# Token stages of a two-layer hybrid block: from a scheduler's order to an order written out, with split work spread over the products

## The chip, the cores and the metric

The kernel runs on one core of one Trainium2 chip. The metric is device time in microseconds of one execution. The program is built through a tile framework: the kernel text emits instructions, the framework's scheduler puts the instructions of each engine into one fixed order, and on the chip each engine issues its own instructions in that order and waits on semaphores for the others. TensorE (PE), VectorE (DVE), ScalarE (ACT) and GpSimd (POOL) compute; the queue of SyncE (SP) issues every transfer.

## The reference, cut to what matters

Two layers of a hybrid block over 1280 tokens (256 of context, 1024 latent) of width 1024. In each layer a normalised and modulated input goes through one input projection, whose columns feed three branches: a bidirectional state-space scan (SSD), grouped-query attention (GQA), and differential attention. The outputs go through one output projection, are normalised and added to the stream.

```python
def ssd_branch(...):
    xs, bs, cs, dt_f, dt_b = prep(p)            # depthwise conv, SiLU, softplus
    y_lf, _ = ssd_scan(xl, dlf, a_f, bl, cl, s_f)                 # chunks of 128 tokens
    y_lb, _ = ssd_scan(flip(xl), flip(dlb), a_b, flip(bl), flip(cl), s_b)
    y = yf + flip(yb_rev) + xs * d_skip[:, None]
    return rmsnorm(y * silu(z), norm_g)
def gqa_branch(...):      # per-head RMSNorm of q and k, axial rotary, softmax attention, SiLU gate
def diff_branch(...):     # rotary on q and k, two softmax maps, o1 - lam * o2, RMSNorm, SiLU gate
```

## The kernel before, in words

The 1280 tokens are ten tiles of 128. Products in float32 accuracy are made of three matmuls: each operand is split into a high part (rounded to fp32r) and a low part (the rest, `lo_part`, L126 to L128), and hi*hi, hi*lo and lo*hi are summed in PSUM.

A layer has these stages, in the order in which they are emitted:

1. Products with channels on partitions for conv inputs (`t_block`, L572), the depthwise conv (`conv_tile`, L599), step sizes (`dt_part`, L492), and splitting of the output weights.
2. The token stages (L909 to L1113), which the change is about. `tok_chunk` (L939) takes one block of columns of the projection, called a chunk of weights here: 0 is z, 1 is dq and dk, 3 is dv (256 columns), 2 is gq, gk and gv, 4 is the gates. For each chunk it loads the eight k-tiles of the weights (L943, three landing buffers `wf`), splits them into `wh` (ACT, L947) and `wl` (DVE for even k, POOL for odd k, L948; nine buffers each), and then, for each token tile, makes 24 matmuls into one of two PSUM banks `prj` (L954 to L960) and works off the bank at once: tanh and a multiply for the SiLU (L963, L964), or a copy (L977), rotary (`rope`, L875), norms (`gqa_norm`, L890), splits (`qk_split`, L825), PE transposes into another bank (`qk_transpose`, L838), an ACT copy out of it (L843) and stores through SP.
3. While chunks 0, 1 and 3 run, the generator `scan` (L753) is advanced by 1.3 steps per full product (`SCR`). For each of ten token tiles it does a forward step and a backward step of the SSD. The forward step loads `ab`, a broadcast of decays (L762, 1 MB, one buffer), makes masked C*B products (L767 to L770), 16 DVE instructions on `ab` (L773, L774), an exponential (L776), eight ACT and eight DVE instructions (L779, L780), one POOL product (L782), eight products (L790), and adds parts; state updates are in `state_step` (L705). The first of the two directions to reach a tile stores its part (`yp`) and the second loads and adds it (L797 to L799, L812 to L816).
4. While chunks 2 and 4 run, `finish` (L731) works off one token tile of the scan's output at every other product: loads, product with z, square sum, root (POOL, L117), four transposes, splits, store.
5. Attention (from L1226), for which `prefetch` emits the first loads of q, k and v (L1106 to L1108) ahead of chunk 4, and then the output projection.

The order of instructions on every engine and on SP's queue is the scheduler's in this kernel: it simulates the program with a timing model and picks by priority what it holds to be ready. The text only proposes an order. An instruction once placed is issued in its place on the chip, whatever the real times are.

## Time and profile before

| | us |
|---|---|
| runs | 2067.94 and 2073.93, median 2070.93 |
| profiled execution, its own time | 2063.46 |
| span of the profiled execution | 2061.6 |
| busy in the span: PE, weight loads | 1806.6, 1471.4 |
| busy in the span: DVE, ACT, POOL | 1428.5, 1041.5, 1211.7 |
| token stages of layer 0, first to last product | 206 to 602 |
| token stages of layer 1 | 1273 to 1614 |

Busy time of an engine is the union of its instructions. A matmul's duration in the trace is its latency, and matmuls overlap, so the distance between starts tells more than the duration. The granted clock is a share of TensorE's full 2.4 GHz; its lower level is 1.2 GHz. A wait row names who waited, for whom, the time in total, how often, and the longest.

### The profile page before, as it was taken

Reading aid. Unit: us, or ns where it says so; the run is one execution under the profiler, and the core shown is the slowest. Engines: PE = TensorE matmul, PEld = TensorE weight load, DVE = VectorE, ACT = ScalarE, POOL = GpSimd, SP = SyncE. Lnnn points to the kernel's source line nnn. Section 1 sums busy time; section 2 is a strip of 40 time slices with the busy share of each in tenths; the row PEclk is TensorE's granted clock in tenths of the full one; section 3 lists DMA queues with packets and bytes.
Section 4 is the critical chain, followed back from the end, with each engine's and each line's share of the span. In section 5 each row is a group of like instructions: output and inputs, shape, how many; then the busy total and the mean of one; then the engine's idle time right before and its main releaser. Section 6 shows DMA issues by size and latency. Waiting matters only on the chain. (4 is left out here: it accounts for less than half of the span.)

```text
span 2061.6 us, 30333 instructions
## 1 busy us (share of the span) xinstructions
PE 1806.6 (88%) x9936; PEld 1471.4 (71%) x9936; DVE 1428.5 (69%) x3286; ACT 1041.5 (51%) x1955; POOL 1211.7 (59%) x1135
## 2 busy tenths in 40 slices
PE   4899989899879999988988799888899899989895
PEld 3677777787668667876775487777777777878783
DVE  4777566766538776698866578468656588788954
ACT  3445233334437775766654345234244477777661
POOL 3626245747616676777755326466567378787761
PEclk9899999899999999998989899999999999999897
DMA  9157546776786788786656138667766866557545
GB/s 290 47 170 271 152 165 191 236 235 176 222 259 198 245 263 257 234 256 202 211 191 214 63 102 280 226 183 231 244 202 204 260 185 192 157 155 237 161 152 205
DMA packets 359998, 418.57 MB, mean 203 GB/s; under 512 B 38753, under 2 KB 252833, under 8 KB 359841
## 3 DMA queue, kind: packets, MB, share of 16 engines
q1 hardware_dynamic: 359840, 416.64, 65.1%
q8 instruction: 78, 1.28, 0.3%
q14 instruction: 80, 0.65, 0.1%
HBM read 282.18 MB, written 134.38 MB: 202 GB/s over the span
## 5 line engine op out<-in xcount | busy, mean ns | idle before, releaser
L128 POOL TENSOR_TENSOR pl<-pf,ph 128x512 fp32r<-128x512 f32 x283 | 373.6, 1325 | 189.0 <-DVE ph L1391 69.7
L1241 DVE TENSOR_SCALAR_CACHE_REDUCE pt<-sc 128x512 f32<-128x512 f32 (+1 forms) x600 | 334.2, 587 | 78.5 <-PE sc L1239 63.4
L958 PE MATMUL prj<-wh,u 128*128 128x512 f32 (+1 forms) x768 | 296.6, 389 | 33.0 <-DVE th L964 18.1
L1254 ACT ACTIVATE pt<-pt,nm 128x1280 f32<-128x1280 f32 x192 | 262.3, 1366 | 92.1 <-DVE nm L1252 91.0
L959 PE MATMUL prj<-wl,u 128*128 128x512 f32 (+1 forms) x768 | 294.8, 384 | 10.3 <-POOL wl L128 7.8
L960 PE MATMUL prj<-wh,u 128*128 128x512 f32 (+1 forms) x768 | 291.7, 380 | 0.0
L1369 PE MATMUL tp<-ident,pt 128*128 128x128 f32 x1312 | 209.3, 285 | 14.0 <-ACT pt L1254 5.6
L1379 ACT COPY pf<-tp 128x512 f32<-128x512 f32 x289 | 166.8, 581 | 74.9 <-PE tp L1369 49.3
L1412 PE MATMUL po<-pl,vt 128*128 128x256 f32 x644 | 183.1, 307 | 15.6 <-POOL pl L128 14.7
L958 PEld LDWEIGHTS prj<-wh,u 128*128 128x128 f32 x768 | 151.8, 199 | 62.5 <-DVE th L964 19.9
L1411 PE MATMUL po<-ph,vt 128*128 128x256 f32 x644 | 186.0, 303 | 5.2 <-DVE ph L1391 2.9
L1369 PEld LDWEIGHTS tp<-ident,pt 128*128 128x128 f32 x1312 | 162.1, 147 | 37.9 <-ACT pf L1379 10.7
L959 PEld LDWEIGHTS prj<-wl,u 128*128 128x128 f32 x768 | 152.0, 198 | 38.0 <-POOL wl L128 11.2
L960 PEld LDWEIGHTS prj<-wh,u 128*128 128x128 f32 x768 | 151.7, 198 | 23.5
L1239 PE MATMUL sc<-dk,q 128*128 128x512 f32 (+1 forms) x400 | 146.1, 408 | 15.2 <-DVE pt L1241 12.0
L1412 PEld LDWEIGHTS po<-pl,vt 128*128 128x128 f32 x644 | 126.3, 196 | 33.0 <-POOL pl L128 25.3
L1411 PEld LDWEIGHTS po<-ph,vt 128*128 128x128 f32 x644 | 127.2, 197 | 19.4 <-DVE ph L1391 5.6
L606 DVE SCALAR_TENSOR_TENSOR cacc<-craw,hw,cacc 128x1284 f32<-128x1284 f32 (+1 forms) x64 | 120.0, 1877 | 28.0 <-ACT cacc L603 12.0
L581 PE MATMUL prj<-u,wTh 128*128 128x512 f32 x256 | 109.8, 429 | 22.2 <-DVE u L209 14.2
L1239 PE MATMUL sc<-gk,q 128*128 128x256 f32 (+1 forms) x400 | 110.0, 385 | 19.9 <-DVE pt L1241 16.7
L342 PE MATMUL ops<-y,wo 128*128 128x512 f32 (+1 forms) x304 | 117.7, 387 | 10.5 <-DMA y<-y 6.3
L582 PE MATMUL prj<-u,wTh 128*128 128x512 f32 x256 | 109.3, 427 | 7.4 <-DVE u L128 6.8
(277 smaller groups left out, 4310.7 us busy)
## 6 DMA issues: line engine op xcount, KB each, us to landing
wo<-wo SPq DMA_DIRECT2D x80, 512.0 KB, 4.9
wm<-in_wmod_dram SPq DMA_DIRECT2D x48, 512.0 KB, 6.2
dk<-dk SPq DMA_DIRECT2D x16, 1280.0 KB, 7.9
ab<-acs SPq DMA_DIRECT2D x18, 1024.0 KB, 7.5
wo<-wos SPq DMA_DIRECT2D x32, 512.0 KB, 3.7
wf<-in_wtok_dram SPq DMA_DIRECT2D x64, 256.0 KB, 4.4
y<-y SPq DMA_DIRECT2D x30, 512.0 KB, 5.7
op<-o SPq DMA_DIRECT2D x48, 256.0 KB, 4.4
```

The source lines that it names most:

```text
L128: eng.tensor_tensor(out_, full, hi.bitcast(F32), op=ALU.subtract)
L606: V.scalar_tensor_tensor(acc[:, a0:1284], raw[:, a0 + j:1284 + j], hw[:, i * 5 + j:i * 5 + j + 1], acc[:, a0:1284], op0=ALU.mult, op1=ALU.add)
L958: TE.matmul(ps[:, c0:], uh, wh[k][:, c0:], start=k == 0, stop=False)
L959: TE.matmul(ps[:, c0:], uh, wl[k][:, c0:], start=False, stop=False)
L960: TE.matmul(ps[:, c0:], ul, wh[k][:, c0:], start=False, stop=k == KT - 1)
L1239: TE.matmul(ps[:, 0:b - a].rearrange("p (t c) -> p t c", c=P), q[:, jb.q0 + j], kt[:, a // P:b // P], start=x == 0, stop=x == len(qq) - 1)
L1241: V.tensor_scalar(ts[r][:, a:b], ps[:, 0:b - a], -1.0, None, op0=ALU.mult, op1=ALU.min, accum_out=mts[r][:, i:i + 1])
L1254: S_.activation(e, e, AF.Exp, bias=nm, scale=-1.0, accum_out=jb.s2[:, j, mp_:mp_ + 1])
L1369: TE.transpose(tp[:, j * P:(j + 1) * P], jb.pt[2 * hf + j % 2][:, cs(2 * s + j // 2)], ident)
L1379: S_.copy(pf[:, :w_], tp[:, :w_])
L1411: TE.matmul(o, vv, a[:, c], start=k == 0, stop=False)
L1412: TE.matmul(o, vv, b[:, c], start=False, stop=k == jb.nk - 1)
```

## The change

- The four compute engines issue the token stages' instructions in the order of the text (`manual_schedule` over PE, DVE, ACT and POOL). SP's order, and where the region's instructions fall among those emitted outside it, stay the scheduler's.
- A product and the working off of its bank are two calls now. `tok_rows` is a generator with several steps; `rest` (after each product) advances the tiles of the last two products by a step or two, so each tile's tail is spread over the next products. The first two token tiles of a chunk are made as a pair, k by k.
- `tok_weights` for the next chunk is emitted within `rest` of the last product of a chunk: half ahead of that product's own evacuation, half behind. Landing buffers `wf` go from 3 to 5, `wh` and `wl` from 9 to 8 each, `tt` from 2 to 3.
- `scan` is written as three steps per token tile, each issued between the matmuls of a product; the next tile's loads come a step or more ahead; `ab` has two buffers. Forward and backward parts go to two scratch tensors, and `finish` adds them.
- `finish` is a generator of eight steps, up to two (chunk 2) or three (chunk 4) of them running. The rotary tables for GQA are made at chunk 2 and no longer at the start.
- The first loads for attention are emitted behind the fifth group of chunk 4, and may not come ahead of that group's store on the queue (`hold`, `behind`).
- `pk` of the two layers shares one buffer.

The core of the diff:

```diff
-SCR = 1.3
+SCD = 2.0
-WB, RB, T2B = 9, 3, 2
+WB, WFB, RB, T2B = 8, 5, 3, 2
...
+            ahead = load(0)
+            back = load_back(0)
+            yield
+            xs = state_in(0, 0, ahead[0])
+            left = None
+            for c, cb in enumerate(CB + (None,)):
+                if c < NT:
+                    xf, ab, bc = ahead
...
+                        if c:
+                            po = y_off((bc[:, 1], bc[:, 3]), Sf)
+                if left:
+                    xl, wl_, yl, cl = left
+                    pd = xpp.tile([P, 8, 64], F32, name="pd", tag="pd")
+                    for h in range(8):
+                        TE.matmul(pd[:, h], wl_[:, h], xl[:, h // 4, h % 4 * 64:h % 4 * 64 + 64],
+                                  start=True, stop=True)
...
+                if c < NT - 1:
+                    ahead = load(c + 1)
+                yield
...
+            def product(ch, group, beside):
+                on(pipe[0])
...
+                for n, (i, k) in enumerate(ks):
+                    while at and at[0] == n:
+                        at.pop(0)
+                        beside.pop(0)()
+                    ps, uh, ul = pss[i], u[k][:, 0, cs(group[i])], u[k][:, 1, cs(group[i])]
+                    TE.matmul(ps[:, c0:], uh, wh[k][:, c0:], start=k == 0, stop=False)
+                    TE.matmul(ps[:, c0:], uh, wl[k][:, c0:], start=False, stop=False)
+                    TE.matmul(ps[:, c0:], ul, wh[k][:, c0:], start=False, stop=k == KT - 1)
...
+            def rest(ck, ch, group, more=None):
+                on(pipe[1])
+                finish_on()
+                on(pipe[1])
+                if more:
+                    next(more)
+                finish_on()
+                done = pipe.pop(0)
+                new = []
+                if group:
+                    pss, c0 = pss_of.pop((ch, group))
+                    new = [tok_rows(ck, ch, ps, t, c0) for ps, t in zip(pss, group)]
+                    on(new)
+                pipe.append(new)
+                if more:
+                    next(more, None)
+                on(done)
...
+            tok_order.enter_context(tc.manual_schedule(engines={E_.PE, E_.DVE, E_.Activation, E_.Pool}))
...
+                seq = [(ch, g) for ch in (0, 1, 3) for g in groups(ch)]
+                units = sum(CW[ch] * len(g) for ch, g in seq) / 512
+                rate, credit = 32 / (units - SCD - 1.0), 0.0
+                for n, (ch, group) in enumerate(seq):
+                    nxt = seq[n + 1][0] if n + 1 < len(seq) else 2
+                    if n >= SCD - 1:
+                        credit += rate * CW[ch] * len(group) / 512
+                    product(ch, group, [lambda: next(sc, None)] * int(credit))
+                    credit -= int(credit)
+                    rest(ck, ch, group, tok_weights(nxt) if nxt != ch else None)
...
+            for n, group in enumerate(groups(4)):
+                if n:
+                    product(4, group, [])
+                finish_new(ck, 3)
+                rest(ck, 4, group)
+                if n == 4:
+                    hold.append(stored[4])
+                    for kind in (0, 1):
+                        prefetch(kind, -1)
+                    vt[(0, 0)] = load_v(d_dv, 0, "dv", 2)
+                    hold.clear()
```

## Rows read from the trace of the kernel before

**Rows 1.** Busy time by stage: layer 0 chunks 0/1/3, 2, 4; layer 1 the same.

```profile
206.00:453.00 247.00, 220.03 (x1143) 187.11 (x1142) 156.51 (x349) 79.73 (x178) 122.08 (x96) 0.92 0.62 191
453.00:523.00 70.00, 65.22 (x319) 52.25 (x318) 43.48 (x94) 29.19 (x71) 50.74 (x59) 1.00 0.66 197
523.00:602.00 79.00, 66.05 (x285) 52.08 (x285) 30.46 (x53) 22.55 (x51) 32.77 (x41) 0.91 0.80 245
1273.00:1498.00 225.00, 191.43 (x1066) 164.24 (x1065) 147.17 (x311) 75.50 (x169) 128.59 (x101) 0.94 0.73 225
1498.00:1557.00 59.00, 56.85 (x281) 46.69 (x281) 33.05 (x69) 25.18 (x62) 43.22 (x55) 0.95 0.63 186
1557.00:1614.00 57.00, 52.88 (x233) 41.72 (x232) 29.01 (x50) 19.92 (x43) 30.08 (x37) 0.91 0.74 218
```

The columns are start:end, length, busy us and (instructions) of PE, weight loads, DVE, ACT and POOL, granted clock, busy share of the DMA engines, GB/s.

**Rows 2.** Single lines of PE in short windows: L958 full and half width, L790.

```profile
L958 PE MATMUL prj<-wh,u x8: 389/389/389, 575.2 to 580.0; 128*128 128x512 f32 x8
...
L958 PE MATMUL prj<-wh,u x9: 282/283/363, 427.9 to 430.9; 128*128 128x256 f32 x9
...
L790 PE MATMUL pd<-xbf,ab x16: 217/275/275, 248.3 to 249.9; 128*128 128x64 f32 x16
```

**Rows 3.** Timeline of PE at 243 us: scan matmuls in a stream.

```profile
243.10 1.03 PE L714 MATMUL stp<-xs,xbb 128*128 128x256 f32 x4
243.97 0.61 PE L767 MATMUL gp<-bct 128*128 128x128 f32 x4
```

**Rows 4.** Lines of PE, 206 to 453 us: the transposes of chunk 1.

```profile
L841 PE MATMUL qps<-identr,st 128*128 128x128 f32 x80 | 11.5, 272 | 4.2 <-DVE st L831 4.0 <-POOL st L128 0.2
```

**Rows 5.** Waits of PE in layer 0, 206 to 605 us: first and last of 15.

```profile
PE prj L958 <- DVE th L964: 11.2, 4, 7.0
...
PE xtp L623 <- DVE cacc L610: 0.2, 1, 0.2
```

**Rows 6.** Waits of PE in layer 1, 1273 to 1620 us: first and last of 14.

```profile
PE po L726 <- DVE yt L728: 11.8, 6, 5.4
...
PE prj L958 <- ACT raw L977: 0.2, 1, 0.2
```

**Rows 7.** Lines of DVE by shape, 206 to 453 us.

```profile
L774 DVE SCALAR_TENSOR_TENSOR ab<-ab,acs 128x128 f32<-128x128 f32 x72 | 29.2, 445 | 0.0
L780 DVE SCALAR_TENSOR_TENSOR ab<-gf,dts,ab 128x128 f32<-128x128 f32 x72 | 25.0, 394 | 0.1
L773 DVE TENSOR_SCALAR ab<-ab,acs 128x128 f32<-128x128 f32 x72 | 22.5, 368 | 28.9 <-DMA ab<-acs 28.9
L728 DVE TENSOR_TENSOR yt<-po,eacs 128x512 f32<-128x512 f32 x15 | 10.2, 683 | 10.8 <-POOL y L795 10.8
L887 DVE TENSOR_TENSOR raw<-raw,rd 128x512 f32<-128x512 f32 x8 | 9.1, 1133 | 0.1
L831 DVE SCALAR_TENSOR_TENSOR st<-raw,st 128x256 fp32r<-128x256 f32 x10 | 8.4, 844 | 7.1 <-ACT st L830 7.1
```

**Rows 8.** One line of DVE, 206 to 453 us: shortest, median and longest.

```profile
L774 DVE SCALAR_TENSOR_TENSOR ab<-ab,acs x72: 332/343/1404, 235.1 to 442.6; 128x128 f32<-128x128 f32 x72
```

**Rows 9.** Lines of POOL by shape, 453 to 523 us (chunk 2).

```profile
L117 POOL TENSOR_TENSOR nrr<-irm,mhalf 128x6 f32<-128x6 f32 x8 | 11.1, 1392 | 0.2
L128 POOL TENSOR_TENSOR st<-raw,st 128x384 fp32r<-128x384 f32 x7 | 7.7, 1104 | 3.2 <-ACT st L834 3.1
...
L888 POOL TENSOR_TENSOR raw<-raw,t 128x256 f32<-128x256 f32 x5 | 3.7, 737 | 5.1 <-DVE raw L884 5.1
...
L795 POOL TENSOR_TENSOR y<-yt,y 128x512 f32<-128x512 f32 x2 | 2.6, 1294 | 1.0 <-DVE y L792 0.9
```

**Rows 10.** Timeline of SP's queue, 570 to 588 us (chunk 4 of layer 0).

```profile
570.62 4.80 SPq L1049 DMA_DIRECT2D dk<-dk  x1
...
580.61 4.70 SPq L1032 DMA_DIRECT2D vt<-dv  x2
...
587.51 0.38 SPq L965 DMA_DIRECT2D gt<-th  x1
```

More of the change, by code (lines that the diff above doesn't have):

```diff
@@ L751, in finish, with finish_on, finish_new, load @@
                          yp.rearrange("p k a t -> p k (a t)").bitcast(F32))
+        def finish_on():
+            for g in list(running):
+                if next(g, 1):
+                    running.remove(g)
+        def finish_new(fp, nb):
+            if todo and len(running) < nb:
+                running.append(finish(todo.pop(0), fp, nb))
+                next(running[-1])
         def scan():
-            half = set()
             Sf = sp.tile([P, 2, 256], F32, name="Sf")
             Sb = sp.tile([P, 2, 256], F32, name="Sb")
-            for c, cb in enumerate((1, 0, 9, 8, 7, 6, 5, 4, 3, 2)):
-                xb = sp.tile([P, 2, 384], F32, name="xbf", tag="xb", bufs=2)
-                SY.dma_start(xb, d_xb[c])
+            CB = (1, 0, 9, 8, 7, 6, 5, 4, 3, 2)
+            def load(c):
+                xf = sp.tile([P, 2, 384], F32, name="xbf", tag="xbf", bufs=2)
+                SY.dma_start(xf, d_xb[c])
+                ab = bc = None
@@ L764, in scan, with load_back @@
-                    SY.dma_start(bc, d_bc[:, :, cs(c)].rearrange("i p t -> p i t"))
-                    pg = xpp.tile([P, 2, P], F32, name="gp", tag="gp")
-                    for g in range(2):
-                        TE.matmul(pg[:, g], bc[:, 2 * g], bc[:, 2 * g + 1], start=True, stop=True)
+                return xf, ab, bc
+            def load_back(c):
+                xb = sp.tile([P, 2, 384], F32, name="xbb", tag="xbb")
+                SY.dma_start(xb, d_xb[CB[c]])
+                ct = None
+                if c and CB[c] >= t0:
+                    ct = sp.tile([P, 2, P], F32, name="ct", tag="ct")
+                    SY.dma_start(ct, d_bc.rearrange("(g b) p t -> b p g t", b=2)[1][:, :, cs(CB[c])])
+                return xb, ct
@@ new lines, in scan @@
+            ahead = load(0)
+            back = load_back(0)
+            yield
+            xs = state_in(0, 0, ahead[0])
[3 more added lines that the diff above has]
+                    xf, ab, bc = ahead
+                    mid = c >= t0
+                    if mid:
+                        pg = xpp.tile([P, 2, P], F32, name="gp", tag="gp")
+                        for g in range(2):
+                            TE.matmul(pg[:, g], bc[:, 2 * g], bc[:, 2 * g + 1], start=True, stop=True)
+                        if c:
[6 more added lines that the diff above has]
+                                  start=True, stop=True)
+                if c < NT and mid:
@@ L788, in scan @@
-                    pd = xpp.tile([P, 8, 64], F32, name="pd", tag="pd")
-                    for h in range(8):
-                        TE.matmul(pd[:, h], W[:, h], xb[:, h // 4, h % 4 * 64:h % 4 * 64 + 64],
-                                  start=True, stop=True)
-                    V.tensor_tensor(y, pd.rearrange("p h d -> p (h d)"), y, op=ALU.add)
-                    if c:
-                        yt = y_off(c, 0, (bc[:, 1], bc[:, 3]), Sf)
-                        G.tensor_tensor(y, yt, y, op=ALU.add)
@@ L820, in scan @@
-                if cb != 2:
-                    state_step(cb, 1, xb, Sb, c == 0)
+                if c < NT - 1:
+                    ahead = load(c + 1)
+                yield
+                if ct is not None:
+                    po = y_off((ct[:, 0], ct[:, 1]), Sb)
+                if cb != 2:
+                    state_step(xb, xs, Sd, Sb)
+                if ct is not None:
+                    yt = y_scale(po, cb, 1)
+                    SY.dma_start(d_yb[cb], yt)
+                if c < NT - 1:
+                    back = load_back(c + 1)
+                    if c + 1 < NT - 1:
+                        xs = state_in(c + 1, 0, ahead[0])
@@ new lines, in on @@
+            def on(gens):
+                for g in gens:
+                    next(g, None)
+            def rest(ck, ch, group, more=None):
[15 more added lines that the diff above has]
+                on(done)
@@ L1015, in block_kernel @@
             todo = [c for c in (1, 0, 6, 5, 7, 4, 8, 3, 9, 2) if c >= t0]
-            with pool("trp2", 4, space=PSUM) as trp_, pool("fin", 2) as fp, pool("wsplit2", 2) as wo_:
-                for t, _ in enumerate(tok_chunk(ck, 2, 0)):
-                    if wtodo:
-                        split_wout(*wtodo.pop(0), wo_)
-                    if t % 2:
-                        finish(todo.pop(0), fp)
+            with pool("trp2", 4, space=PSUM) as trp_, pool("fin", 2) as fp, pool("rot2") as rp2:
+                tb = tables(rp2)
+                next(tb)
+                seq = groups(2)
+                for n, group in enumerate(seq):
+                    if n % 2 == 0 and n < 7:
+                        finish_new(fp, 2)
+                    product(2, group, [])
+                    rest(ck, 2, group, tok_weights(4) if n == len(seq) - 1 else None)
+                    if n == 0:
+                        next(tb, None)
+                product(4, groups(4)[0], [])
+                while running or pipe[0] or pipe[1]:
+                    rest(ck, 2, None)
+                    on(pipe[0])
         ps_.close()
```

320 lines of the change are left out of this document (174 added, 146 removed).

## The prediction

> **What bounds the kernel now.** I read the page first (PE is by far the busiest engine), then the table of windows cut at the token stages, then PE's products and scan matmuls one by one, then PE's waits, then DVE, POOL and SP in the stages where PE waits.
>
> The token stages take 737 us of the span, and PE shows as busy for 84 to 96% of each [rows 1]. That share overstates the work, since it counts latencies. In a clean stretch the eight k-steps of a product start 0.686 us apart (575.2 to 580.0 in seven steps), so a full product costs 8 x 0.686 = 5.5 us; a half-wide one costs 8 x 0.375 = 3.0 us [rows 2]. A scan tile costs PE 1.7 us for its 16 `pd` instructions [rows 2], 0.87 us for each direction's state product and 0.44 us for C*B [rows 3]; the two `y_off` have the state product's shape, so I take 0.87 us for each. Together 1.7 + 4 x 0.87 + 0.44 = 5.6 us. The transposes of chunk 1 are at most 11.5 us in ten products [rows 4].
>
> From this a floor for PE in each stage:
>
> - Layer 0, chunks 0, 1, 3: 20 x 5.5 + 10 x 3.0 + 10 x 5.6 + 11 = 207 us, where 247 are taken.
> - Layer 0, chunks 2 and 4: 20 x 5.5 + 10 for transposes (an estimate after rows 4) = 120, where 149 are taken.
> - Layer 1, chunks 0, 1, 3 (eight z products, eight full and two half of chunk 1, ten of dv, eight full scan tiles and two with state products only): 16 x 5.5 + 12 x 3.0 + 8 x 5.6 + 2 x 1.7 + 10 = 182, where 225 are taken.
> - Layer 1, chunks 2 and 4: 16 x 5.5 + 2 x 3.0 + 8 = 102, where 116 are taken.
>
> The slack is 40 + 29 + 43 + 14 = 126 us. Of it the waits of PE are 45 us in layer 0 (15 rows) and 40 us in layer 1 (14 rows) [rows 5, 6]; the other 41 us are stretches at the lower clock level, 1.2 GHz (the mean granted clock is 0.91 to 0.95 in five of the six stages [rows 1]), and latencies of small matmuls with nothing behind them. So PE's floor is the bound, and what is to be had are bubbles: PE waiting for a bank that ACT and DVE have not emptied (`th`, `raw`), for split weights at the head of a chunk, and for the scan's VectorE steps.
>
> **The change part by part.**
>
> *Scan.* Before, `ab` has one buffer, so its 1 MB load begins only when the tile before is done; DVE waits 28.9 us for it in chunks 0, 1 and 3 of layer 0 [rows 7]. After, it is loaded a tile ahead. The arithmetic stays: the add of `yp` moves from the scan into `finish` on POOL, at 1.3 us each [rows 9], as often as before. DVE's work per tile is 8 x (0.406 + 0.347 + 0.313) = 8.5 us by busy time over count, two `yt` at 0.68 us, and five more of about that size or less (two state adds, the add of `pd`, two masks at an estimated 0.4): 8.5 + 1.4 + 2.9 = 12.8 us [rows 7]. The pace is 32 steps over 22 units in layer 0, so a tile of three steps per 2.06 products. In chunk 1 a product costs DVE 1.14 (L887) + 0.84 (L831) + two half-wide ones, estimated at 0.45 each, = 2.9 us [rows 7]. So per tile DVE needs 12.8 + 2.06 x 2.9 = 18.8 us, and PE 2.06 x (5.5 + 1.1) + 5.6 = 19.2 us. That is a tie: in chunk 1 there is no room for an order that is only nearly right. In chunks 0 and 3 DVE needs some 2 us less per tile than PE.
>
> I take half of the slack for chunks 0, 1 and 3: 22 us in layer 0 (bounds -10 and 40) and 23 us in layer 1 (bounds -10 and 43). The lower bounds are the same gain with each of a layer's 32 scan steps 1 us late.
>
> *Heads of chunks.* The splits of the next weights are emitted inside the last product's tail, four ahead of its own evacuation. With 8 instead of 9 buffers each, a split must wait until the last product has read that k-tile; the pair of products that follows takes 6 x 0.229 = 1.4 us per k-step, against the 0.69 us of a single one [rows 2], so later splits have time to come. This gain lies in the sums of the stages, and isn't added again.
>
> *Chunks 2 and 4.* In layer 0 they take 70 + 79 us [rows 1]. In chunk 2 POOL is busy 51 of the 70 us, more than DVE, with a root of 1.39 us, a split of 1.10 and a rotary add of 0.74 in each product [rows 9]. What moves away from there is the scan's end; what comes are the added sum in `finish` (four times 1.3 us) and the rotary tables, four more products on POOL. I take the two as equal, and chunk 2 as staying near 68 to 70 us: here POOL is close behind PE. Chunk 4 has little on any engine but PE (DVE 30, ACT 23, POOL 33 of 79 us [rows 1]), so with its tail spread it can come to 62. I take 17 us for layer 0 (bounds 0 and 29) and 3 us for layer 1 (bounds -8 and 14), where PE already is busy 57 of 59 us in chunk 2.
>
> *Attention loads.* In layer 0 SP issues four large loads from 570.6 us on, and the gate's store comes out only at 587.5 [rows 10]; its `th` buffer is then not free, and PE's longest wait for it is 7.0 us [rows 5]. After, the loads stand behind the fifth group's store. But four products of layer 0 still follow it, and nothing puts their stores ahead of the loads, so I count 3 us of that wait as staying. In layer 1 only two products follow (11 us), while the issue alone took some 17 us in layer 0 [rows 10]; the first loads are for the first job, so attention starts on them, and I count 3 us lost (bounds 0 and 10).
>
> *The shared `pk`.* Layer 1's constants are loaded after layer 0's last use, in layer 0's attention, which covers it: nothing. If it weren't hidden, it is one small load.
>
> **A rule weighed.** One line of DVE, 128x128 from two SBUF operands, takes 332 ns at best, 343 in the median and 1404 at worst [rows 8]: in some of its executions it is held. The Trainium skill (SBUF — State Buffer, "Who interferes with whom") says that a VectorE instruction with two SBUF inputs and a GpSimd instruction that reads SBUF exclude each other for the whole instruction. The trace agrees in kind. By that rule a denser stage has more collisions, which speaks against the change. By the present averages, which hold the collisions of today, the sum below stands; with more of them it is that of the second rival.
>
> **The sum.** 22 + 23 + 17 + 3 - 3 = 62 us. The profiled execution took 2063.5 us, so 2001.5 by its own time. It lies 7.5 us under the median of the runs, which I add again: 2009 us.
>
> **The rivals.**
>
> 1. *The pipeline reaches the floor.* If PE's waits go almost wholly, the clock stays up too, and three quarters of the slack come back: 95 us, 1968.5 + 7.5 = 1976 us. For it: both what PE waits for and the `ab` load are things that the change treats. Against: the tie on DVE in chunk 1. Chance 0.2.
> 2. *DVE becomes the bound of chunks 0, 1 and 3.* POOL is busy 122 of 247 us there [rows 1]. Packed into 225 us, its share goes from 0.49 to 0.54. DVE's four lines with the rotary and scan work are on average 20 to 30% over their best already (445 against 332 ns, rows 7 and 8). If DVE's 18.8 us per tile grow to 22, ten tiles and eight tiles lose about 3 us each: 18 x 3 = 54 us of which the slack left over takes some 12, so the gain falls by 42 to 20 us: 2051 us, within 2%. For it: the tie. Against: before, DVE is busy 157 of 247 us there, with room. The case in which SP's order, still the scheduler's, keeps feeding the pipeline late ends in the same place. Chance 0.22.
> 3. *A fixed order stalls PE (slower).* Some 64 scan steps stand between product matmuls on PE; each has a matmul that needs a result of DVE or POOL from the step before, and when it is late, the products behind it wait too. The largest waits of this kind already show, 5.4 us at `y_off` in layer 1 [rows 6]. If each step waits x us, the change loses 64x: the gain is gone at x = 62 / 64 = 1.0 us, and over 2% are lost at x = (62 + 41) / 64 = 1.6. At 2 us: 2009 + 128 = 2137 us. Against: the lag between a step and the next is some 4 to 6 us of matmuls, since a step comes about every 0.7 products, and the result of POOL's product of W and D is used only two steps after it is emitted. Chance 0.13.
>
> The forecast itself has 0.45, with an own range of 1985 to 2030.
>
> **How the numbers follow.** The measurement of this kernel can tell about 2% (41 us) from no change. Faster by over 2%, under 2030: the forecast and rival 1, 0.45 + 0.2 = 0.65. Within 2%: rival 2, 0.22. Slower: rival 3, 0.13. The range goes from 1962 (rival 1 with 85% of the slack) to 2066 (rival 2 with no gain but 5 us), and leaves out rival 3 and a little below.
>
> **What would show it.** Right: token stages of some 675 us in place of 737; DVE's wait for `ab` nearly gone; PE's waits under 45 us in both layers together, with none over 5 us at the gate; a granted clock of 0.96 or more there; chunk 1 still the stage with the largest waits of PE on DVE; attention's time unchanged. Wrong: PE waits of 1 us and more at most of the scan's matmuls (rival 3); DVE busy over 90% in chunk 1 with longer durations on the same lines (rival 2); or a gain that shows in the token stages and is lost again at attention's first scores, behind late loads.

## The result and the profile after

The changed kernel takes 2135.06 us (two runs, 2135.03 and 2135.09) against 2070.93: ratio 1.031, 95% interval 1.0246 to 1.0374, so slower, where I had forecast 2009 us. The profiled execution has a span of 2133.3 us at a mean granted clock of 0.923 (2061.6 at 0.937 before). PE, DVE, ACT and POOL are busy 1822.2, 1437.7, 1032.4 and 1193.6 us, each within 2% of before: the work is nearly the same, its placing isn't.

The windows by stage, with the columns of [rows 1] (chunks 0/1/3, 2 and 4 of layer 0, then of layer 1):

```profile
198.00:468.00 270.00, 233.87 (x1185) 199.62 (x1185) 173.43 (x378) 82.19 (x192) 113.02 (x92) 0.91 0.60 187
468.00:540.00 72.00, 59.98 (x286) 47.77 (x284) 43.75 (x82) 28.97 (x69) 53.40 (x68) 0.96 0.51 144
540.00:625.00 85.00, 65.51 (x270) 52.80 (x271) 25.76 (x40) 18.47 (x40) 31.57 (x36) 0.82 0.78 232
1299.00:1557.00 258.00, 206.55 (x1107) 176.67 (x1105) 160.41 (x320) 76.93 (x177) 119.75 (x98) 0.89 0.66 206
1557.00:1621.00 64.00, 53.62 (x258) 43.03 (x258) 39.97 (x79) 24.87 (x64) 49.24 (x69) 0.96 0.48 137
1621.00:1682.00 61.00, 51.19 (x219) 41.39 (x219) 19.21 (x30) 15.02 (x33) 24.40 (x28) 0.88 0.67 204
```

All six stages are longer than in [rows 1]: 23, 2 and 6 us in layer 0, 33, 5 and 4 us in layer 1. Together 810 us against 737, so 73 us; the spans differ by 72, and nothing outside the token stages has changed much. PE's busy share fell: 234 of 270 us in layer 0's chunks 0, 1 and 3, where it was 220 of 247.

I cut each stage further at the first matmul of each chunk's first product. Chunk 1 stands out: 129 us where it was 104 in layer 0, and 120 where it was 96 in layer 1, while chunk 3 became shorter in layer 0 (49 for 58) and chunk 4 longer (90 for 79). These are not the same pieces of work, though: five of the scan's tiles fall into chunk 1 in the change, in either layer, and four before. What the order costs in chunk 1 is read below against e1, which has the change's work there. Chunk 1 of layer 0 in one window, in the change and before:

```profile
285.00:414.00 129.00, 108.40 (x484) 90.15 (x484) 87.34 (x188) 38.39 (x93) 64.43 (x53) 0.85 0.59 178
291.00:395.00 104.00, 90.82 (x432) 74.72 (x432) 67.03 (x158) 38.08 (x88) 57.42 (x46) 0.92 0.68 200
```

In the change DVE is busy 68% of it, POOL half, ACT 30%, and the granted clock is 0.85: no engine is full. PE's waits in layer 0 (198 to 628 us) come to 68 us where they were 45 [rows 5], and in layer 1 to 72 where they were 40 [rows 6]. The largest in layer 0, then the largest of ACT in the same stretch, and ACT's waits for the same 16 DVE instructions before (206 to 605 us):

```profile
PE prj L1109 <- DVE th L1042: 16.5, 3, 10.8
PE po L735 <- DVE yt L740: 11.5, 3, 4.8
PE qps L916 <- POOL st L128: 10.4, 6, 2.3
...
ACT ab L857 <- DVE ab L855: 81.8, 8, 13.8
...
ACT ab L779 <- DVE ab L774: 36.4, 21, 6.2
...
ACT ab L776 <- DVE ab L774: 8.3, 2, 8.0
```

Before, these waits were 36.4 us at the weightings of W (L779) and 8.3 us at the exponential (L776). In the change it is the scan's exponential (L857) that stands in ACT's order and waits for DVE's 16 instructions on `ab`, and whatever ACT has behind it waits too. What that means in time can be followed through one scan tile. The timeline of all engines in chunk 1 of layer 0 (start, duration, engine, instruction; in brackets the idle time before it and what ended it):

```profile
360.22 1.06 ACT L857 ACTIVATE ab<-ab 128x1024 f32<-128x1024 f32 x1 [12.30 <-DVE ab L855]
...
363.60 2.45 ACT L873 ACTIVATE ab<-gf,dts 128x128 f32<-128x128 f32 x8
...
364.38 4.82 DVE L874 SCALAR_TENSOR_TENSOR ab<-gf,dts,ab 128x128 f32<-128x128 f32 x8
...
369.27 2.84 POOL L880 TENSOR_TENSOR ab<-ab 128x1024 f32<-128x1024 f32 x1 [1.28 <-DVE ab L874]
369.90 2.77 DVE L962 TENSOR_TENSOR raw<-raw,rd 128x512 f32<-128x512 f32 x1
...
372.74 1.26 POOL L963 TENSOR_TENSOR raw<-raw,t 128x512 f32<-128x512 f32 x1 [0.63 <-DVE raw L962]
374.04 0.42 ACT L905 ACTIVATE st<-raw 128x256 fp32r<-128x256 f32 x1 [5.47 <-POOL raw L963]
...
374.49 0.43 DVE L906 SCALAR_TENSOR_TENSOR st<-raw,st 128x256 fp32r<-128x256 f32 x1 [1.82 <-ACT st L905]
...
375.43 0.68 DVE L740 TENSOR_TENSOR yt<-po,eacs 128x512 f32<-128x512 f32 x1
...
376.25 1.65 PE L735 MATMUL po<-Sf,bct 128*128 128x256 f32 x4 [3.73 <-DVE yt L740]
...
377.70 3.51 PE L838 MATMUL pd<-xbf,ab 128*128 128x64 f32 x16
...
381.25 0.69 DVE L847 TENSOR_TENSOR y<-pd,y 128x512 f32<-128x512 f32 x1 [2.62 <-PE pd L838]
...
386.65 1.06 ACT L857 ACTIVATE ab<-ab 128x1024 f32<-128x1024 f32 x1 [11.90 <-DVE ab L855]
387.62 0.56 ACT L1054 COPY raw<-prj 128x512 f32<-128x512 f32 x1
```

From one exponential to the next each step follows within some two microseconds of the last, on whichever engine it lies. The eight weightings of W go ACT, DVE, POOL. DVE's rotary multiply (L962) runs beside POOL's product and takes 2.77 us in place of 0.69. The rest of the rotary goes POOL, ACT, and back to DVE's split L906. Behind that split, in DVE's order, stands `yt`, which empties the only `po` bank; PE waits 3.73 us for it, and with it the next product. Then come `pd`, its sum on DVE, the 16 instructions on `ab` (to 386.6) and the next exponential, with the copy out of PE's bank behind it. That is 26.4 us per tile, through all four engines, though DVE works 18.2 of 26 us in that stretch. Ten products take about five such tiles.

PE's wait for `yt` has a second price. The windows just behind its three waits of this kind in the chunk (they end at 349.4, 376.3 and 402.7 us), and one ahead of the middle one:

```profile
350.00:357.50 7.50, 7.50 (x27) 6.65 (x26) 3.23 (x10) 0.00 (x0) 1.78 (x2) 0.50 0.44 146
361.10:372.50 11.40, 11.40 (x58) 9.52 (x56) 9.52 (x14) 6.26 (x17) 8.28 (x6) 1.00 0.57 153
376.20:383.30 7.10, 7.04 (x26) 6.30 (x27) 3.24 (x9) 0.00 (x0) 2.42 (x3) 0.53 0.37 115
403.00:410.00 7.00, 7.00 (x25) 6.20 (x25) 2.74 (x8) 0.00 (x0) 2.00 (x3) 0.50 0.36 104
```

PE worked at the full clock up to the wait, stood for 3.0 to 4.8 us, and then ran near the lower level (0.50 to 0.53) for some 7 us. `pd` falls into these 7 us: it takes 3.5 us in these three tiles and 1.89 in the chunk's first two.

The same three tiles have one more thing in common: a rotary multiply that takes 2.8 us in place of 0.69 (see the last section). The chunk's first two tiles have no rotary ahead of their `pd`, and PE doesn't wait for `yt` there. No run takes away the multiply's 2.1 us by themselves, so their part in the wait isn't shown.

### The profile page after: what moved, and what is told of

Its sections match the earlier page's. It is cut to its first block, busy times and chain, and to the rows that moved or that the text cites. A ratio compares the mean times of both kernels' runs of the same rounds, so it can differ in the third digit from the quotient of the medians.

```text
span 2133.3 us, 30302 instructions
## 1 busy us (share of the span) xinstructions
PE 1822.2 (85%) x9936; PEld 1486.1 (70%) x9936; DVE 1437.7 (67%) x3286; ACT 1032.4 (48%) x1955; POOL 1193.6 (56%) x1135
## 5 line engine op out<-in xcount | busy, mean ns | idle before, releaser
L1109 PE MATMUL prj<-wh,u 128*128 128x512 f32 (+1 forms) x768 | 308.4, 402 | 42.0 <-DVE th L1042 23.7
L1110 PE MATMUL prj<-wl,u 128*128 128x512 f32 (+1 forms) x768 | 296.6, 386 | 18.1 <-DVE wl L128 10.8
L1111 PE MATMUL prj<-wh,u 128*128 128x512 f32 (+1 forms) x768 | 293.5, 382 | 0.0
L1538 PE MATMUL tp<-ident,pt 128*128 128x128 f32 x1312 | 208.8, 283 | 12.2 <-ACT pf L1548 6.3
L1109 PEld LDWEIGHTS prj<-wh,u 128*128 128x128 f32 x768 | 156.6, 204 | 71.5 <-DVE th L1042 24.7
L1110 PEld LDWEIGHTS prj<-wl,u 128*128 128x128 f32 x768 | 157.0, 204 | 46.5 <-DVE wl L128 12.3
L1111 PEld LDWEIGHTS prj<-wh,u 128*128 128x128 f32 x768 | 156.0, 203 | 26.0
L1408 PE MATMUL sc<-dk,q 128*128 128x512 f32 (+1 forms) x400 | 143.0, 409 | 20.5 <-DVE pt L1410 14.3
L1581 PEld LDWEIGHTS po<-pl,vt 128*128 128x128 f32 x644 | 126.7, 197 | 44.3 <-POOL pl L128 33.3
```

Of the source, the lines that this page charges most:

```text
L1109: TE.matmul(ps[:, c0:], uh, wh[k][:, c0:], start=k == 0, stop=False)
L1110: TE.matmul(ps[:, c0:], uh, wl[k][:, c0:], start=False, stop=False)
L1111: TE.matmul(ps[:, c0:], ul, wh[k][:, c0:], start=False, stop=k == KT - 1)
L1408: TE.matmul(ps[:, 0:b - a].rearrange("p (t c) -> p t c", c=P), q[:, jb.q0 + j], kt[:, a // P:b // P], start=x == 0, stop=x == len(qq) - 1)
L1538: TE.transpose(tp[:, j * P:(j + 1) * P], jb.pt[2 * hf + j % 2][:, cs(2 * s + j // 2)], ident)
L1581: TE.matmul(o, vv, b[:, c], start=False, stop=k == jb.nk - 1)
```

## The experiments

Medians are shown with their ratio to the kernel before on the same chip (its medians were 2065 to 2069 us in the experiments, 2070.9 in the result). Differences in us below are of medians, partly of two chips, so a few us in them say nothing. "Chunk 1" and "token" are lengths in us, layer 0 and layer 1, cut as above; "order" names the engines held to the order of the text.

| run | median | ratio, 95% | chunk 1 | token |
|---|---|---|---|---|
| kernel before | 2070.9 | 1 | 104, 96 | 396, 341 |
| the change (order: all four) | 2135.1 | 1.031 (1.0246 to 1.0374) | 129, 120 | 427, 381 |
| e1, no order | 2047.5 | 0.9907 (0.9873 to 0.9941) | 105, 113 | 374, 343 |
| e2, all but ACT | 2102.8 | 1.0177 (1.0148 to 1.0206) | 123, 116 | 408, 364 |
| e6, all but DVE | 2108.7 | 1.0192 (1.0169 to 1.0215) | 113, 119 | 408, 370 |
| e15, all but PE | 2139.2 | 1.0364 (1.0328 to 1.04) | 125, 119 | 436, 378 |
| e16, all but POOL | 2142.3 | 1.0378 (1.0343 to 1.0413) | 128, 127 | 425, 383 |
| e17, ACT and DVE | 2146.6 | 1.0365 (1.0339 to 1.0392) | 127, 122 | 439, 378 |
| e18, ACT | 2080.8 | 1.0055 (1.0036 to 1.0074) | 106, 122 | 384, 352 |
| e5, PE | 2080.1 | 1.0053 (1.003 to 1.0076) | 115, 112 | 400, 356 |
| e12, all four, chunks 0, 1, 3 only | 2111.2 | 1.0216 (1.0199 to 1.0233) | 129, 121 | 401, 372 |
| e3, exponential later | 2124.5 | 1.0273 (1.0247 to 1.0299) | 125, 121 | 420, 375 |
| e7, e3 and banks first | 2141.5 | 1.0345 (1.0315 to 1.0374) | 131, 128 | 428, 383 |
| e11, one step per product | 2152.7 | 1.0417 (1.04 to 1.0435) | 90, 76 | 434, 388 |
| e13, split later | 2176.4 | 1.0546 (1.0511 to 1.0581) | 149, 146 | 446, 402 |
| e4, loads last | 2145.2 | 1.0377 (1.0351 to 1.0404) | 129, 120 | 413, 382 |
| e8, no order, loads early | 2066.3 | 0.9994 (0.9978 to 1.001) | 106, 113 | 388, 352 |
| e9, before with held loads | 2062.3 | 0.9984 (0.9969 to 0.9998) | 103, 87 | 385, 344 |
| e14, before with buffers | 2053.2 | 0.9934 (0.9912 to 0.9955) | 102, 87 | 383, 340 |
| e10, before with both | 2039.5 | 0.9882 (0.9863 to 0.99) | 102, 90 | 374, 337 |

**Is it the order?** e1 takes the one line away:

```diff
-            tok_order.enter_context(tc.manual_schedule(engines={E_.PE, E_.DVE, E_.Activation, E_.Pool}))
```

> Everything of the change is kept, but no engine is held to the order of the text; the scheduler orders all engines. Theory (the fixed order is what costs: PE, DVE and ACT each stand behind a late instruction): about 64 us over the kernel before come back and part of the gain from early loads and spread tails shows, so 2020 to 2070 us. Rival (the new layout of the work itself costs, by the later attention loads, fewer weight buffers and the scan in three steps): it stays at 2110 to 2140 us.

The time falls by 88 us, below the kernel before. Everything else in the change is therefore worth a gain of about 1%, and the fixed order costs 4%. By stage, cut as above, chunks 0, 1 and 3 take 461 us in both layers together, where the change has 515 and the kernel before 464; chunks 2 and 4 take 255, where the change has 294 and the kernel before 273. So the order costs some 54 and 38 us, and the gain of the other parts lies almost wholly in chunks 2 and 4.

In the windows of e1 chunk 1 of layer 0 has the same work on DVE in 24 us less; then chunk 1 of layer 1, in the change and in e1:

```profile
287.00:392.00 105.00, 94.83 (x485) 79.82 (x484) 90.21 (x182) 36.55 (x88) 66.19 (x54) 0.95 0.65 193
...
1371.00:1491.00 120.00, 96.07 (x501) 81.01 (x500) 95.34 (x195) 37.91 (x94) 69.30 (x56) 0.91 0.62 188
...
1309.00:1422.00 113.00, 98.99 (x511) 83.73 (x511) 93.88 (x184) 34.08 (x87) 73.47 (x60) 0.92 0.66 201
```

In layer 0 DVE is busy 86% there (68% in the change), at a granted clock of 0.95 (0.85). PE's waits in the chunk are 10 us, where the change has 20.5; by this the other 14 of the 24 us go with the lower clock (an estimate: length less waits is 95 and 109 us for the same matmuls). In layer 1 the order costs chunk 1 only 7 us: most of what it takes over the 96 before is there without the order too.

**Which engine's order?** Seven runs differ in that one set of engines; the line of e17:

```diff
+            tok_order.enter_context(tc.manual_schedule(engines={E_.DVE, E_.Activation}))
```

> As the change, but ScalarE is left to the scheduler; PE, DVE and POOL keep the order of the text. Theory A (the exponential stands on ACT ahead of the copy that empties PE's bank, 82 us of ACT waits in layer 0): most of the loss comes back, 2070 to 2095 us. Theory B (the stall is DVE's own order, rotary split ahead of the scan's yt, which holds the single bank of y_off and so PE): little comes back, 2115 to 2140 us.

> As the change, but DVE is left to the scheduler; PE, ACT and POOL keep the order of the text. Freeing ACT gave back 32 of the 88 us that freeing all gave. Theory (DVE's order is the larger part: its 16 instructions on ab stand ahead of the adds that free the scan's single banks): 2060 to 2090 us. Rival (ACT's order is the main one, DVE's worth little): 2110 to 2130 us.

> As the change, but only PE keeps the order of the text; DVE, ACT and POOL are left to the scheduler. Theory (PE only suffers what the three others do late in their own order): near the version with no order at all, 2045 to 2070 us. Rival (scan matmuls fixed between the products stall PE whatever the others do): 2095 to 2130 us.

> The changed kernel with DVE, ACT and POOL held to the order of the text and PE left to the scheduler. Freeing ACT alone gave 2103 us, freeing DVE alone 2109, from 2135; PE alone in order gave 2080. Theory A (the loss needs the whole ring: an order is bad where a late link on one engine holds work behind it that the next engine waits for, so any one engine freed gives back a part): 2095 to 2115 us. Rival B (PE's own order is the cause, since PE is the bound and each scan matmul in it blocks products; the other three only add to it): near 2050 to 2075, the time of the kernel with no order plus little. Rival C (the cause lies in the order of ACT, DVE and POOL among themselves): 2125 to 2140.

> The changed kernel with PE, DVE and ACT held to the order of the text and POOL left to the scheduler. Theory A (every engine is a link): some gain, but smaller than with ACT or DVE free, since PE's waits on POOL are the short ones (st, xs): 2115 to 2130 us. Rival C (one of the waits on POOL, the state input xs or the split st, is a main link): under 2110 us. No gain (2130 to 2145) says that POOL's order costs nothing here.

> The changed kernel with DVE and ACT alone held to the order of the text, PE and POOL left to the scheduler. Freeing PE alone and POOL alone gave nothing (2139 and 2142 us), freeing ACT or DVE alone gave 32 and 26. Theory C (the loss lies in the order of ACT and DVE between themselves: the two that empty PE's banks): 2120 to 2140 us, the time with all four held. Rival A (the ring of all four: with two of its four engines free the loss falls by half or more): 2075 to 2100.

> The changed kernel with ACT alone held to the order of the text. Theory C1 (an exponential waiting on ACT in front of the copies out of PE's banks costs by itself, whatever the other engines' order): 2075 to 2100 us. Rival C2 (ACT's order costs only together with DVE's, since it is DVE's own fixed place of its 16 instructions that makes the exponential late): 2045 to 2065 us, as with no order.

Freeing ACT gives 32 us and freeing DVE 26; freeing PE or POOL gives nothing. (e2, e6 and e5 came out between the ranges of their two theories.) Holding ACT and DVE alone costs the whole loss (2147 us, over the range given for it), holding ACT alone a third of it (33 us over e1). So the order of ACT and DVE is enough for the loss, and the orders of PE and POOL are not needed for it. I take it that each of the two has a place where it waits for the other and keeps something behind that place which the other, or PE, needs. That is argued, since DVE alone was not held: what DVE's order costs without ACT's stays open. The traces point to DVE in layer 0's chunk 1, the stage that loses most: all runs of these that hold DVE's order have it at 123 to 129 us, all that don't at 105 to 115 (in e15 and e17 with 24 and 15 us of the waits for loads that are told of below). The prices don't add up engine by engine either: with DVE free 61 us remain over e1, about the 33 of PE alone and the 33 of ACT alone together, and with ACT free 55 remain.

I had expected a ring of all four (e15: 2095 to 2115) and was wrong. PE's order is not free: held alone, with the other three fitted around it, it costs 33 us (e5). But when ACT and DVE are held, PE's own order adds nothing. One caveat: with PE free the scheduler places the C*B products early, and in layer 0 PE waits for their loads (`gp` for `bct`: 33.3 us in e15, 21.8 in e17, 3.0 in the change), which may hide a gain there. In layer 1 that wait is 3.3 and 2.2 us, and the token stages still take 378 us in both, 381 in the change. The wait rows of ACT, layer 0, 198 to 640 us, in e17:

```profile
ACT ab L857 <- DVE ab L855: 73.3, 6, 16.9
```

and in e18:

```profile
ACT ab L857 <- DVE ab L855: 52.9, 6, 14.9
```

In e1 the row has 36.0 us. With ACT alone in order the same exponential waits long, but chunks 0, 1 and 3 take 235 and 220 us, no more than in e1 (239 and 222). ACT's 33 us lie elsewhere: chunks 2 and 4 take 281 us for 255, and the stretch between the layers' token stages 687 for 677. The median is in the range of theory C1, but the exponential is not what costs it.

**Where in the region?** e12 ends the order ahead of chunk 2:

```diff
+            tok_order.close()
             sc_.close()
...
-        tok_order.close()
```

> As the change, with the order of the text on four engines in chunks 0, 1 and 3 only; chunks 2 and 4 are the scheduler's. The stages of the version with no order are shorter by 27 + 27 us in chunks 0, 1 and 3 and by 27 + 11 us in chunks 2 and 4. If these parts add, 2095 to 2105 us; if the loss of the later chunks is only handed on from the scan's, 2110 to 2135 us.

Of the 88 us, 24 come back, less than the 30 to 40 expected if the parts add. By stage they do add: chunks 2 and 4 take 255 us in both layers together, as in e1 (294 in the change), and chunks 0, 1 and 3 518 (515 in the change). But the stretch between the layers' token stages is 13 us longer (688 for 675), and why was not followed.

**One wait at a time.** e3 takes the exponential, and W's weightings, out of ACT's way: they are emitted behind the next copy out of PE's bank.

```diff
-                    S_.activation(D, D, AF.Exp)
+                    late.append(lambda D=D: S_.activation(D, D, AF.Exp))
...
                     on(new)
+                run_late()
```

> As the change, all four engines in the order of the text, but the scan's exponential, and the ACT and DVE step on W if it falls into the same product, are emitted behind the evacuation of that product. Theory A: the same part comes back as with ACT left free, 2075 to 2100 us. Theory B: DVE's steps come later still, so 2125 to 2150 us.

The wait rows of ACT in layer 0, 199 to 620 us:

```profile
ACT th L1052 <- PE prj L1122: 78.3, 17, 10.1
ACT raw L1065 <- PE prj L1122: 66.5, 12, 12.0
```

The 81.8 us are gone, ACT now waits for PE, and the median is 11 us lower; the intervals of the two ratios overlap. A large row of waits was no measure of what it cost. In the timeline above the copy at 387.62 was ready only some 2.5 us before, since its product ended with a matmul that started at 384.75.

e7 adds to e3 that the forward state's matmul and add go ahead of DVE's 16 instructions, so that its bank comes free sooner:

```diff
+                Sd = state_decay(c, 0, Sf) if 0 < c < NT - 1 else None
+                if c < NT - 1:
+                    state_step(xf, xs, Sd, Sf)
                 if mid:
...
-                if c < NT - 1:
-                    state_step(xf, xs, Sd, Sf)
```

> All four engines in the order of the text, with two moves: the forward state's decay, product and add are emitted ahead of DVE's 16 instructions on ab, so that the bank of the state product is free before them; and, as in the run with the late exponential, ACT's exponential stands behind the evacuation. Theory (banks held behind DVE's 16 instructions cost PE 6 us at a time in layer 1, 19 + 12 us of waits there): PE's waits at the state product fall to under 8 us in layer 1, and 20 to 35 us come back over the late exponential alone: 2090 to 2105 us. Rival (the lag moves elsewhere in DVE's queue): 2115 to 2130 us.

It is 17 us slower than e3. PE's wait for `po`, behind `yt`, rises from 12.2 to 18.2 us in layer 0, and the one for the state input `xs` in layer 1 is 19.7 us, as in the change (19.2). That the 16 instructions, now later, are the longer chain is my reading and was not followed further.

e13 puts the rotary's split (L905, L906), which stood ahead of `yt` in the tile above, a step later, behind the scan's:

```diff
                     yield
+                    yield
                     if konly:
...
+                on(post)
+                del post[:]
                 on(pipe[0])
...
+                early = of.pop(id(done), None) == 1
+                if early:
+                    on(done)
```

> As the change, all four engines in the order of the text, but in chunk 1 the split of a token tile is emitted a step later, behind the scan's step in place of ahead of it, and its transposes at the head of the next product. In the change DVE waits 17.3 us in 115 for this split (its rotary goes DVE, POOL, ACT and back to DVE with nothing between), and the scan's instructions stand behind it. Theory (the ping-pong of neighbours in a fixed order makes chunk 1 slow, not the amount of work): DVE's wait for it falls under 6 us, chunk 1 falls by 15 to 20 us in each layer, 2095 to 2112 us. Rival (the time goes to the next link of the scan's chain, product pd and the single banks): chunk 1 stays within 6 us, 2122 to 2140 us.

DVE's wait for ACT at that split, 17.3 us in eight times in the change, is 0.2 us, and chunk 1 is 20 and 26 us longer. The waits of PE and of DVE, 285 to 434 us:

```profile
PE qps L916 <- DVE st L906: 26.8, 7, 6.8
...
DVE Sb L729 <- PE stp L725: 19.9, 4, 6.3
DVE Sf L729 <- PE stp L725: 13.2, 3, 4.6
```

Now PE waits at the transposes for the late split, and DVE waits for the state product that stands behind them on PE. My theory for this run fell: the split is not a cause that can be moved out of the way, the chain only closes at another link.

e11 slows the scan to one step per product, the rest following behind chunk 3:

```diff
-                    product(ch, group, [lambda: next(sc, None)] * int(credit))
-                    credit -= int(credit)
+                    steps = min(1, int(credit))
+                    product(ch, group, [lambda: next(sc, None)] * steps)
+                    credit -= steps
```

> As the change, all four engines in the order of the text, but never more than one scan step inside a product; what is left of the scan runs behind chunk 3 with no products beside it. Theory (two steps in one product put the backward y_off's bank and DVE's 16 instructions in front of PE, ACT's evacuation and the next rotary): chunk 1 falls from 129 to 105 to 112 us in layer 0, and the scan's rest costs some 25 to 40 us behind chunk 3, so 2110 to 2140 us in all. Rival (any fixed place of a step stalls): chunk 1 stays over 120 us and the whole is over 2145 us.

Chunk 1 falls to 90 and 76 us, below the kernel before, with less of the scan in it (DVE works 64 us there in layer 0, 87 in the change). But what is left of the scan costs 52 and 58 us more behind chunk 3, where it has no products beside it, and the whole is longer than expected. So it is the pace of 1.45 steps per product (1.6 in layer 1) that the order of chunk 1 can't carry, and at one step per product the scan doesn't fit into the three chunks.

**Chunk 4 and the attention loads.** e4 emits the loads behind the last group, e8 is e1 with the loads ahead of chunk 4 and no hold.

```diff
-                if n == 4:
+                if n == len(groups(4)) - 1:
```

> As the change, but the first attention loads stand behind the last group's store of chunk 4 and no longer behind the fifth's. PE waits 11 us for the gate's buffer at the end of layer 0 and 7 to 10 us in layer 1 because stores stand on SP behind these loads. Theory (those stalls are the loads' price): 15 to 20 us come back, 2115 to 2120 us. Rival (the loads then start later and attention's first scores wait as long): 2130 to 2145 us.

> No engine held to the order, and the first attention loads are emitted ahead of chunk 4 without a hold, as in the kernel before; the rest of the change is kept. If holding the loads is worth something by itself, this is slower than the version with no order at all, 2055 to 2065 us; if the hold only moves the wait from the gate's stores to attention's first scores, it is the same, 2042 to 2052 us.

In e4 layer 0's chunk 4 gets 13 us shorter (77 for 90), but the stretch to layer 1's first token product 17 longer (692 for 675): attention's first scores wait. The waits of PE in e4, 540 to 640 us:

```profile
PE sc L1408 <- DMA q<-gq: 11.9, 1, 11.9
PE prj L1109 <- DVE th L1042: 6.4, 1, 6.4
```

In the change, the second row is 16.1 us and the first isn't there. With free engines the hold behind the fifth group is worth 12 us in each layer's chunk 4 and costs 10 us once between the layers (e8 against e1). The medians differ by 19 us, a few more than these add up to.

**Parts of the change in the kernel before.** e9 takes the held loads into the kernel before (behind the sixth gate tile's store), e14 the buffers, e10 both:

```diff
-WB, RB, T2B = 9, 3, 2
+WB, RB, T2B = 8, 3, 2
...
-                    wf = wk.tile([P, 512], F32, name="wf", tag="wf", bufs=3)[:, 0:w_]
+                    wf = wk.tile([P, 512], F32, name="wf", tag="wf", bufs=5)[:, 0:w_]
...
+                if t == 5:
+                    hold.append(stored[4])
+                    for kind in (0, 1):
+                        prefetch(kind, -1)
+                    vt[(0, 0)] = load_v(d_dv, 0, "dv", 2)
+                    hold.clear()
```

> The kernel before with one part of the change: the first attention loads are emitted behind the store of the sixth gate tile and may not come ahead of it on SP's queue. Theory (the hold is the one part that gains, 19 us in the layout without an order): 2045 to 2055 us. Rival (the hold pays only where finish and the products are spread as in the change): 2062 to 2075 us.

> The kernel before with the buffers alone (five landing buffers, eight split buffers), the attention loads as before. With the hold alone the ratio was 0.998, with hold and buffers 0.988. If the buffers are what gains: 2040 to 2050 us. If the two only gain together (the heads of chunk 4 and the loads use the same queue): 2055 to 2068 us.

> As the run before it, with the change's buffers for split weights as well: five landing buffers in place of three, eight split buffers in place of nine. If the wait for landed weights (31 us of ACT in layer 0) is on PE's path at the heads of chunks, 5 to 12 us less than the run before it; if PE's wait there is for DVE and POOL, the same within 4 us.

Together they give 1.2%, 23 us less than the hold alone where I had expected 5 to 12, and the lowest median of all runs; e1, which has the new pipeline too, is no better (its interval overlaps). e14 came out between its two ranges. Its waits of PE for the gate's buffer, 199 to 585 us, where [rows 5] has 11.2 us:

```profile
PE prj L960 <- DVE th L966: 1.9, 1, 1.9
```

## Why the prediction was wrong

- *The step that failed* is "I take half of the slack for chunks 0, 1 and 3": 22 and 23 us less were forecast, 23 and 33 us more were measured, both outside the bounds that I had given (a loss of 10 at most). Two things are wrong in it. The larger is the price of the written order, which the sum put at nothing: 54 us in these chunks (e1). The other is the gain itself: with the order taken away, it is 3 us of the 45. The forecast rested on the sums per tile, 18.8 us of DVE and 19.2 of PE. The first of them was near: 18.2 us in the tile shown, 2.1 of it by the multiply that is held beside POOL. But a sum of work is a tile's length only if the fullest engine always has something ready. Under the written order the tile's length in layer 0's chunk 1 is the chain through it, and that is 26.4 us. I had said that the tie left "no room for an order that is only nearly right", and then took half of the slack for it all the same, without following the written order from one instruction to the next.
- *The reason against rival 3* was that a step has 4 to 6 us of matmuls before the next. That looked at PE alone. The chain crosses from DVE to POOL to ACT to DVE between two scan matmuls, and the queues of DVE and ACT carry the rotary work between its links.
- *Rival 3* (2137 us at 2 us per step, chance 0.13) has the right side, and 1.97 us per step by its formula, (2135 - 2009) / 64. Its kind is right too: an instruction that waits in a fixed order. Its place was wrong: it had PE's order stall products, and with PE free the time is the same (e15), while the order of ACT and DVE alone gives all of it (e17). Its sign was not there either: PE shows waits at 15 of the scan's matmuls in both layers, where some 64 steps were meant. And by the stages 38 us of the loss lie in chunks 2 and 4, where no scan steps are (e1, e12). What it describes exists in part: PE's order alone costs 33 us (e5). That its time came within 2 us of the measured one is luck.
- *Rival 2* (DVE as the bound) is refuted: DVE's share in chunk 1 is 68%, and without the order it rises to 86% in a shorter stage. Its mechanism, DVE's lines held beside POOL, is there in layer 0, for one line on the chain: see below. Of its two numbers, 445 over 332 ns is 34%, not 20 to 30.
- *The `ab` load* did what I said: DVE's 28.9 us of waiting for it [rows 7] are gone; one wait of 4.2 us at that line is for `xbf`. What it was worth by itself is not shown, since the time went into the chain. That two buffers alone would have helped the kernel before wasn't tried.
- *Chunks 2 and 4*: 70 us forecast for chunk 2 of layer 0 and 72 measured. Chunk 4 was to come to 62 and took 85 in that window. Without the order and with the hold it is 72, in e10 64. Over both layers chunks 2 and 4 gain 18 us in e1, where 20 were forecast: the gain is there, but with engines free.
- *Attention loads*: the sum counted 3 us lost for them. The hold is worth 19 us with free engines (e8 against e1), and only 0.2% in the kernel before (e9).
- *Heads of chunks* were not counted on their own. The buffers alone are worth 0.7% in the kernel before (e14).
- *Attention unchanged*: right, 675 us between the layers' token stages against 671.
- *What would show it*: stages of 675 us (810), PE's waits under 45 us (141), clock of 0.96 (0.85 in layer 0's chunk 1), no wait over 5 us at the gate (10.8) all came out wrong; the wait for `ab` and attention's time came out as said. One small slip: 85% of the slack gives 1964 us, not 1962, as the lower end of the range.

What stays open: the share of each link in chunk 1, the held multiply's among them, and what DVE's order costs alone. e3, e7 and e13 each removed one named wait or moved one, and most of the time moved to the next. That the order of ACT and DVE is enough for the loss is shown; a better order for these two was not found.

## What to carry to other kernels

Before work is put into a written order, follow one period of it from an instruction to the same instruction one tile later, across all queues, and compare that chain with the sum of work of the fullest engine; where a period has 18 us of work on DVE and the chain through it is 26, moving single waits won at most 11 us of 88 here, and a slower pace only moved the work. If an order must be held, hold the engines one by one and in pairs: here PE or ACT alone cost 1.5% over no order, and ACT with DVE all of the loss (DVE alone is the one to try next). Compare stages only where they hold the same work: set beside the kernel before, chunk 1 of layer 1 seemed to lose 24 us, and 7 of them came from the order. Try the small parts of a large change in the old kernel too: five landing buffers and loads held behind a store gave 1.2% there, no less than the whole pipeline without its order.

## What the runs showed of the hardware

The same rotary multiply on DVE (128x512, two SBUF operands, eight executions in a layer) takes very different times. Its shortest, median and longest in the change, layer 0 and then layer 1:

```profile
L962 DVE TENSOR_TENSOR raw<-raw,rd x8: 691/1702/2774, 330.3 to 427.6; 128x512 f32<-128x512 f32 x8
...
L962 DVE TENSOR_TENSOR raw<-raw,rd x8: 691/693/694, 1418.9 to 1512.4; 128x512 f32<-128x512 f32 x8
```

and in e1, the same:

```profile
L962 DVE TENSOR_TENSOR raw<-raw,rd x8: 672/678/2282, 324.9 to 402.4; 128x512 f32<-128x512 f32 x8
...
L962 DVE TENSOR_TENSOR raw<-raw,rd x8: 675/683/2286, 1337.8 to 1431.0; 128x512 f32<-128x512 f32 x8
```

The median of 1702 ns stands for no execution: in layer 0 of the change every second one takes 0.69 us and the others 2.71 to 2.77. In the tile shown the multiply started 0.63 us after POOL's product of W and D (369.27, 2.84 us) and ended half a microsecond behind it, and the other three long ones started as soon after that product. The Trainium skill (SBUF — State Buffer, "Who interferes with whom") says that a VectorE instruction with two SBUF inputs and a GpSimd instruction that reads SBUF share one read port, which one of them holds for its whole duration. The timeline agrees with it. Over both layers the order doesn't hold the multiply more often: four of 16 take over 0.9 us in the change, five in e1. What the written order does is to repeat: in layer 0 the same two instructions meet in the same place of every second step of the rotary, on the chain, and in layer 1 never.

A pause of PE costs more than its length here. After the three waits of 3.0 to 4.8 us in layer 0's chunk 1 the granted clock is 0.50 to 0.53 for some 7 us, with PE busy throughout, where it had been 1.00.
